# A hybrid encoder layer: pacing the merges' loads, pausing the convolutions, and masking on GpSimd

## The chip, the cores and the metric

The kernel runs on one core of one Trainium2 chip. The metric is the device time in microseconds of one execution. Engines are called PE (TensorE, with its weight loads shown apart as PEld), DVE (VectorE), ACT (ScalarE), POOL (GpSimd) and SP (SyncE, which issues nearly all DMAs here).

## The reference: one encoder layer over two sequences

A prompt of 1024 tokens and a sample of 2048 tokens, each with 16 learned meta tokens in front, go through one layer with a model width of 1024:

```
xn   = rmsnorm(h, g_pre)
proj = xn @ w_in + b_in            # 6672 columns: q, k, v, z of the attention; q/k, v, z, o, gates of the mLSTM; merge gates
ya   = (neighbourhood_attention(na_q, na_k, na_v, na_rpb) * silu(na_z)) @ w_a
yb   = (mlstm(silu(conv3(ml_qk)), ml_v, ml_g, ml_o) * silu(ml_z)) @ w_b
y    = (sigmoid(mg_a) * ya + sigmoid(mg_b) * yb) @ w_out
out  = h + rmsnorm(y, g_post)
```

The attention looks at a window of 8 rows by 16 columns on a grid 64 columns wide, and at the meta tokens. The mLSTM is a gated recurrence, run forwards and backwards, computed here in chunks of 128 tokens with a triangular mask inside a chunk: for the forward direction a key position s counts for a query position t where s <= t, for the backward direction where s >= t. A depthwise convolution of three taps precedes its q and k. All is float32.

## The kernel before: a dense stream and a sparse stream, interleaved by hand

**Products.** Float32 accuracy comes from splitting each operand into a high part (float32r) and the rest; a product is three matmuls, high x high, high x low, low x high (`mm3`, L178 to L182). So nearly every operand goes once through ACT (the high part, a copy) and once through DVE (the rest, a subtraction): weights L283 and L284, activations L526 and L527, branch outputs L1980 and L1964.

**Order.** The order of PE's instructions is the order in which the Python program issues them. Two generators make it: `dense` walks through `PLAN` (input projections, then six finals), and `sparse` through `STEPS` (mLSTM of the prompt, attention of the prompt, mLSTM of the sample, attention of the sample). `run` advances them in turn by estimated costs. The order of the other engines' instructions, and of SyncE's DMA issues, is found by the framework's scheduler from simulated times; an instruction may float forward when its inputs are ready early. `behind` pins an instruction behind everything issued before it on the same engine. On the chip each queue is worked off in order.

**The seven-product stage.** The prompt's remaining columns are computed by a seven-product scheme in place of eight block products (`sstream`; the first operands are loaded in `sbegin` while the last ordinary projection job runs, in `group`). Its products are numbered 1 to 7 and come in the order 1, 6, 5, 2, 7, ... Between the products `beside` is called once per turn: it advances the convolutions of the mLSTM's q and k (`pstep` advances one of two active `cprep` generators: a load L1579, an ACT pass L1584, DVE passes L1587, a tanh L1589, a DVE pass L1591, a store L1597), background work, and stores of split activations. The prompt's 32 convolution pieces are queued at the third job of the first projection group.

**The mLSTM.** Per head, states are computed over all blocks of 256 tokens, then outputs (`ml_outputs`). For each block a tile `um` is loaded two blocks ahead (L1758, broadcast from DRAM), `mask` adds the triangular mask of 0 and -1e30 to it on DVE (L1780, 128 x 512 elements, both directions), and `decay` takes its exponential on ACT (L1786). The prompt has 4 blocks a head, the sample 8, with 4 heads each.

**The finals.** Each of the six finals takes 512 tokens: two of the prompt, four of the sample. A final has a merge (eight output tiles, each with a product for either branch, L180 to L182 with `yh` and `yl`, then the gates: L2033 to L2037) and an output projection (`prods`, L2066 to L2068: 4 column groups x 2 halves x 4 token tiles, 32 steps). The branch outputs are eight tiles of 256 KB: `yload` loads them (L1960), and splits one at a time, seven of its own turns after the load at the earliest. It is started in the output projection of the final before, after the sixth step, and advanced once a step. In its first turn it issues every load whose data exist. The gate tiles `tg` (256 KB, L2005) are loaded for three output tiles when a merge begins, and from then on three tiles ahead; they have four buffers for each branch. Neither kind of load is pinned. Beside the finals runs the sample's attention, whose `na_prep` loads queries, keys (`kr`, L1343 and L1344), values (`vr`, L1348 and L1349) and biases for each head on the same queue, with one buffer for `kr` and one for `vr`.

## Time and profile before

| | us |
|---|---|
| median of 3 runs | 2712.46 |
| lowest and highest run | 2709.28, 2717.65 |
| the profiled execution | 2722.07 |
| its span, first to last instruction | 2720.3 |
| PE busy | 2674.3 |
| DVE busy | 1791.8 |
| ACT busy | 1547.3 |
| POOL busy | 125.3 |
| seven-product stage begins | 202 |
| sample's mLSTM | 1424 to 1973 |
| finals | 1999 to 2712 |
| sample's attention | 2021 to 2629 |

The profile is one execution. A busy time is the union of an engine's instructions; matmuls are pipelined, so a busy PE may still run below its best. The chain of waits follows the work that ended last backwards, at each step to what released it; a row has its start, its duration and what it was. In rows of windows the figures behind the span's length are the busy times of PE, PEld, DVE, ACT and POOL with their counts of instructions, then the granted TensorE clock, the mean busy share of the core's 16 DMA engines, and what they moved in GB/s. A row of waits has the total, the number of times and the longest. A row of one tile's instructions has the shortest, median and longest duration in ns, and the first and last start in us.

### The profile page before, as it was taken

What the parts mean: (1) busy time and instruction counts of PE and PEld (TensorE: products, weight loads), DVE (VectorE), ACT (ScalarE), POOL (GpSimd) and SP (SyncE); (2) the same over time, 40 slices, a digit from 0 to 9 for tenths busy, and PEclk for the clock granted to TensorE, in tenths of its full rate; (3) what the DMA queues carried; (4) which work ended last, traced back from release to release, by engine and by line L of the source; (5) the groups of instructions that cost most, each with busy time, mean ns of one, the idle gap of its engine ahead of it and who ended that gap; (6) DMA issues with size and microseconds to landing.
All of it is one profiled execution on the core that took longest, in us unless ns stands there. A gap on an engine that the chain in (4) does not pass through costs nothing.

```text
span 2720.3 us, 47309 instructions
## 1 busy us (share of the span) xinstructions
PE 2674.3 (98%) x16504; PEld 2380.2 (87%) x16504; DVE 1791.8 (66%) x4424; ACT 1547.3 (57%) x3471; POOL 125.3 (5%) x294
## 2 busy tenths in 40 slices
PE   9999999999999999999999999999999999999998
PEld 7999988879998789998878888888889898889888
DVE  5547765535777747775424858575768868687764
ACT  5233354435566656666534857575758677677641
POOL 0005000005000014000000000000000000000000
PEclk9999999999999999999999999999999999999999
DMA  9884454369765797756486656785599989798955
GB/s 371 336 283 141 139 188 157 102 238 342 268 228 184 241 320 222 230 183 226 155 287 192 224 201 214 266 284 188 175 335 335 310 270 291 237 328 245 306 202 220
DMA packets 351219, 657.26 MB, mean 242 GB/s; under 512 B 53412, under 2 KB 158580, under 8 KB 350980
## 3 DMA queue, kind: packets, MB, share of 16 engines
q1 hardware_dynamic: 343716, 645.19, 71.3%
q0 software_dynamic: 7264, 9.04, 1.2%
q8 instruction: 130, 2.13, 0.3%
q14 instruction: 109, 0.89, 0.1%
HBM read 438.38 MB, written 215.66 MB: 240 GB/s over the span
## 4 chain that ended last, share of the span: by engine, by line
PE 84%; DMA 9%; DVE 4%; ACT 2%; issue 1%; SPq 0%; POOL 0%; DVEq 0%; ACTq 0%; POOLq 0%
PE pj L180 14%; PE pj L181 13%; PE pj L182 13%; PE pj L658 5%; PE pj L659 5%; PE pj L660 5%; PE sm L1424 2%; PE pj L2066 2%; PE pj L2068 2%; PE pj L2067 2%; PE tr L1410 2%; DMA wraw<-wu 1%; DMA tg<-gt 1%; DMA vr<-nv 1%; PE pa L1852 1%
## 5 line engine op out<-in xcount | busy, mean ns | idle before, releaser
L180 PE MATMUL pj<-xh,whi 128*128 128x512 f32 (+1 forms) x1480 | 580.8, 392 | 5.2 <-ACT st L581 3.9
L181 PE MATMUL pj<-xl,whi 128*128 128x512 f32 (+1 forms) x1480 | 566.2, 383 | 0.4 <-DVE xl L357 0.4
L182 PE MATMUL pj<-xh,wlo 128*128 128x512 f32 (+1 forms) x1480 | 565.3, 382 | 0.2 <-DVE wlo L284 0.2
L658 PE MATMUL pj<-whi,xh 128*128 128x256 f32 (+1 forms) x1152 | 330.8, 287 | 0.0
L182 PEld LDWEIGHTS pj<-xh,wlo 128*128 128x128 f32 x1480 | 278.5, 188 | 58.1 <-DVE wlo L284 0.4
L180 PEld LDWEIGHTS pj<-xh,whi 128*128 128x128 f32 x1480 | 278.5, 188 | 55.0 <-ACT st L581 4.7
L659 PE MATMUL pj<-wlo,xh 128*128 128x256 f32 (+1 forms) x1152 | 324.9, 282 | 0.0
L660 PE MATMUL pj<-whi,xl 128*128 128x256 f32 (+1 forms) x1152 | 324.8, 282 | 0.0
L181 PEld LDWEIGHTS pj<-xl,whi 128*128 128x128 f32 x1480 | 279.0, 189 | 46.4 <-issue 0.7
L2066 PE MATMUL pj<-whi,mh 128*128 128x256 f32 x768 | 221.9, 289 | 0.0
L2067 PE MATMUL pj<-wlo,mh 128*128 128x256 f32 x768 | 218.4, 284 | 0.0
L2068 PE MATMUL pj<-whi,mlo 128*128 128x256 f32 x768 | 218.4, 284 | 0.0
L658 PEld LDWEIGHTS pj<-whi,xh 128*128 128x128 f32 x1152 | 217.2, 189 | 0.4
L659 PEld LDWEIGHTS pj<-wlo,xh 128*128 128x128 f32 x1152 | 217.1, 188 | 0.2
L660 PEld LDWEIGHTS pj<-whi,xl 128*128 128x128 f32 x1152 | 217.1, 188 | 0.0
L1413 DVE TENSOR_TENSOR pts<-tr,pts 96x384 fp32r<-96x384 f32 (+2 forms) x192 | 118.6, 618 | 65.4 <-ACT pts L1412 64.6
L180 PE MATMUL pj<-yh,whi 128*128 128x512 f32 x384 | 154.1, 401 | 0.7 <-ACT yh L1436 0.7
L181 PE MATMUL pj<-yl,whi 128*128 128x512 f32 x384 | 151.0, 393 | 0.2 <-DVE yl L1437 0.2
L182 PE MATMUL pj<-yh,wlo 128*128 128x512 f32 x384 | 151.0, 393 | 0.0
L2067 PEld LDWEIGHTS pj<-wlo,mh 128*128 128x128 f32 x768 | 147.6, 192 | 1.0
L2066 PEld LDWEIGHTS pj<-whi,mh 128*128 128x128 f32 x768 | 147.6, 192 | 1.0
L2068 PEld LDWEIGHTS pj<-whi,mlo 128*128 128x128 f32 x768 | 147.4, 192 | 0.0
(460 smaller groups left out, 6150.8 us busy)
## 6 DMA issues: line engine op xcount, KB each, us to landing
whi<-wh SPq DMA_DIRECT2D x140, 512.0 KB
wlo<-wl SPq DMA_DIRECT2D x140, 512.0 KB
wraw<-wu SPq DMA_DIRECT2D x64, 512.0 KB
wh<-whi SPq DMA_DIRECT2D x64, 512.0 KB
wl<-wlo SPq DMA_DIRECT2D x64, 512.0 KB
gt<-st SPq DMA_DIRECT2D x96, 256.0 KB
tg<-gt SPq DMA_DIRECT2D x96, 256.0 KB
xt<-xt SPq DMA_DIRECT2D x32, 512.0 KB
```

The source lines that it names most:

```text
L180: mm(out, ah, bh, start=start, stop=False, **more)
L181: mm(out, ah, bl, start=False, stop=False, **more)
L182: mm(out, al, bh, start=False, stop=stop, **more)
L658: nc.tensor.matmul(o, xh, wh, start=k == 0 and not (pair and a), stop=False, skip_group_check=True)
L659: nc.tensor.matmul(o, xh, wl, start=False, stop=False, skip_group_check=True)
L660: nc.tensor.matmul(o, xl, wh, start=False, stop=k == KT - 1, skip_group_check=True)
L1410: nc.tensor.transpose(pt[:ks, ch, :], pr_[:, ch * ks:(ch + 1) * ks], self.ident)
L1413: nc.vector.tensor_tensor(pts[:ks, :nb, 1, :], pt[:ks, :nb], pts[:ks, :nb, 0, :].bitcast(F32), op=ALU.subtract)
L1424: nc.tensor.matmul(av[:, cb % 2], vt[:ks, kc // 8 + ch].rearrange("p a b -> p (a b)"), pts[:ks, ch].rearrange("p a b -> p (a b)"), start=c ...
L2066: nc.tensor.matmul(o, mh[:, f, xs], q, start=fresh and f == 0, stop=False, skip_group_check=True)
L2067: nc.tensor.matmul(o, mh[:, f, xs], w[1][:, k, :], start=False, stop=False, skip_group_check=True)
L2068: nc.tensor.matmul(o, ml[:, f, xs], q, start=False, stop=f == KT - 1, skip_group_check=True)
```

## The change

Three edits:

- The convolutions pause: `quiet` is set when the last projection job before the seven-product stage begins, and cleared at the first product 7; while it is set, `beside` advances no convolution.
- The mask of the sample's mLSTM (`s` is 1) is made by two selections on POOL, one for either direction, 2 x 128 elements per partition each, which write -1e30 where the position lies outside the triangle. The prompt's mask stays an addition on DVE.
- `yload` pins its loads and issues at most one per turn, at every second turn, unless the merge already needs it (`need`). Gate tiles are pinned as well; the first three output tiles' six gate tiles of a following final are asked for in the second half of the output projection before it, one at every second step. The first final has none asked for ahead and loads them when its merge begins, as before.

```diff
     def beside(self):
 
         self.turn += 1
-        self.pstep()
-        if (1, 0) in self.have:
+        for _ in range(0 if self.quiet else 1 + ((1, 0) in self.have)):
             self.pstep()
...
             if u == 7 and not n:
+                self.quiet = False
                 self.sbload(1)
...
                 elif last and nxt and nxt[0] == "S":
                     if hf == 0:
+                        self.quiet = True
                         while self.bg:
...
         def mask(b):
             if b < NB:
-                self.behind(nc.vector.tensor_tensor(ums[b], ums[b], self.trim, op=ALU.add))
+                if not s:
+                    self.behind(nc.vector.tensor_tensor(ums[b], ums[b], self.trim, op=ALU.add))
+                    return
+                for d in range(2):
+                    u = ums[b][:, :, d]
+                    nc.gpsimd.affine_select(u, u, [[0, CB], [1 - 2 * d, P]], ALU.is_ge, -BIG, base=0, channel_multiplier=2 * d - 1)
...
         def load(k):
-            nc.sync.dma_start(yl[:, k].bitcast(F32), self.YA[s][b][k][:, :] if k < 4 else self.YB[s][k - 4][:, b * n:(b + 1) * n])
+            self.behind(nc.sync.dma_start(yl[:, k].bitcast(F32), self.YA[s][b][k][:, :] if k < 4 else self.YB[s][k - 4][:, b * n:(b + 1) * n]))
             todo.append((k, step + 7))
...
         while todo or late or half is not None:
+            idle = True
             for k in tuple(late):
                 if (("ml", s) if k > 3 else ("na", s, b, k)) in self.done:
-                    late.remove(k)
-                    load(k)
+                    idle = False
+                    if step % 2 == 0 or self.need:
+                        late.remove(k)
+                        load(k)
+                    if not self.need:
+                        break
             if half is not None:
                 low(half)
                 half = None
-            idle = True
...
-        tgs = {}
+        tgs, self.tgs = self.tgs, {}
+
+        def gate(tgs, ft, br, s, t0):
+            tg = fp.tile([P, n], F32, name="tg", tag=("st", "stT")[br], bufs=4)
+            self.behind(nc.sync.dma_start(tg, self.GT[s][8 * br + ft][:, t0:t0 + n]))
+            tgs.setdefault(ft, []).insert(0, tg)
 
         def gates(ft):
-            if ft < KT:
-                tgs[ft] = []
+            if ft < KT and ft not in tgs:
                 for br in (1, 0):
-                    tg = fp.tile([P, n], F32, name="tg", tag=("st", "stT")[br], bufs=4)
-                    nc.sync.dma_start(tg, self.GT[s][8 * br + ft][:, t0:t0 + n])
-                    tgs[ft].insert(0, tg)
+                    gate(tgs, ft, br, s, t0)
...
+        ahead = deque((ft, br) for ft in range(3) for br in (1, 0)) if nxt and nxt[0] == "f" else ()
         for cq in range(4 if nxt else 2):
...
                     if hook:
                         next(hook, None)
+                    if ahead and cq > 1 and tt % 2:
+                        gate(self.tgs, *ahead.popleft(), nxt[1], n * nxt[2])
                     yield 12 * C256
```

More of the change, by code (lines that the diff above doesn't have):

```diff
@@ L144, in __init__ @@
         self.hold, self.early = deque(), True
-        self.rpre, self.xhold = {}, True
+        self.rpre, self.xhold, self.quiet, self.tgs = {}, True, False, {}
     def rsqrt8(self, pool, v, shape):
```

## The prediction, on record before the result

> **What bounds the kernel now.** I read the page first, then the waits of PE, the chain of waits, the windows, and the rows of the tiles that the change touches. The page says that TensorE is the bound:
>
> ```profile
> span 2720.3 us, 47309 instructions
> ...
> PE 2674.3 (98%) x16504; PEld 2380.2 (87%) x16504; DVE 1791.8 (66%) x4424; ACT 1547.3 (57%) x3471; POOL 125.3 (5%) x294
> ```
>
> The matmuls are the same before and after, in the same order, so an edit can only shorten what PE loses: its idle time, 2720.3 - 2674.3 = 46.0 us, and time at a reduced clock. Part of that is the opening and the end, which no edit touches. The largest idle times are in the last third, where the six merges and output projections run beside the second neighbourhood attention. Waits of PE between 2180 and 2600 us (total, times, longest):
>
> ```profile
> PE sm L1424 <- ACT prb L1393: 7.0, 2, 5.7
> PE sm L1424 <- DVE pts L1413: 3.5, 1, 3.5
> PE sm L1424 <- DVE yg L1431: 2.2, 2, 2.0
> ```
>
> All three stand before the attention's last product. ACT and DVE are only the last links; the chain of waits shows what held them (start, duration, what):
>
> ```profile
> 2177.90 8.15 DMA yl<-yb
> 2186.11 7.41 DMA kr<-nk
> 2193.54 8.33 DMA vr<-nv
> ...
> 2209.74 1.13 PE sm L1424 x4
> ...
> 2322.12 8.37 DMA kr<-nkm
> ...
> 2337.39 1.01 PE sm L1424 x3
> ...
> 2566.05 5.39 DMA tg<-gt
> 2571.46 10.47 DMA vr<-nv
> ...
> 2584.02 0.74 PE sm L1424 x4
> ```
>
> Each time the attention's next keys or values (kr, vr) land late, behind loads for the next merge (yl, its branch outputs; tg, its gates). The queue at the first of the three, as SyncE issued it, and the load on the DMA engines early and late in that projection (the last two figures are DMA share and GB/s):
>
> ```profile
> 2174.72 3.49 SPq L1960 DMA_DIRECT2D yl<-yb  x4
> 2179.19 2.52 SPq L1960 DMA_DIRECT2D yl<-ya  x3
> 2182.76 0.45 SPq L1342 DMA_DIRECT2D qr<-nq  x1
> 2183.39 2.14 SPq L2005 DMA_DIRECT2D tg<-gt  x3
> ```
>
> ```profile
> 2170.00:2191.00 21.00, 21.00 (x172) 20.66 (x171) 15.76 (x37) 16.97 (x38) 0.00 (x0) 1.00 1.03 362
> 2191.00:2213.00 22.00, 20.00 (x151) 19.60 (x150) 13.78 (x32) 15.94 (x37) 0.00 (x0) 0.93 1.00 291
> 2213.00:2236.00 23.00, 23.00 (x188) 22.71 (x187) 16.03 (x37) 19.04 (x43) 0.00 (x0) 1.00 0.79 234
> ```
>
> Seven yl loads and three tg loads leave within 11 us, right when the projection starts, and its first two thirds run with the DMA engines full; the last third has a fifth to spare. After each stall the clock is lowered (the figure before the DMA share):
>
> ```profile
> 2209.80:2213.20 3.40, 3.40 (x16) 3.40 (x17) 1.65 (x4) 2.22 (x7) 0.00 (x0) 0.50 0.77 302
> 2336.10:2342.90 6.80, 5.51 (x25) 5.51 (x26) 5.10 (x13) 6.16 (x18) 0.00 (x0) 0.50 0.90 264
> 2585.30:2588.70 3.40, 3.40 (x17) 3.37 (x16) 2.83 (x6) 2.95 (x9) 0.00 (x0) 0.50 1.01 323
> ```
>
> At half clock half of the stretch is lost: (3.4 + 6.8 + 3.4) / 2 = 6.8 us. The three stalls cost 5.7 + 3.5 + 2.0 = 11.2 us, so together 18.0 us are at stake here.
>
> **Part 1, the merges' loads.** The bytes stay. Each yl load is now pinned behind what was traced on SyncE before it, and one goes at every second turn of the loader's generator instead of all at once. That generator is advanced once in each of an output projection's 32 steps from the sixth on. By the windows above a projection takes about 66 us, so a step is 2.06 us and the eight loads leave over 15 steps, some 31 us, instead of at once. Six gate tiles go, pinned too, in the projection's second half, at every second step. So kr and vr of the attention share the engines with one 256 KB load per 4 us and no longer queue behind ten. What is late next: the last yl load leaves at turn 14, its split is due at turn 21 and ends at 22, of 27 (0 to 26); four steps, 8 us, are left, and the loads quoted land in 5 to 11 us, well inside the 7 turns (14 us) allowed. The gates needed first were asked for 30 us ahead. The cost of the moved loads is hidden by the spare fifth of the last third. Pinning puts nothing new in front of the weights, but a gate tile later in the merge can no longer slip ahead of an attention load that waits for its buffer; it is asked for three tiles ahead. Bounds: 0, if the attention's loads stay late by themselves, to -18.0 us. I take two thirds, **-12.0 us**, because the three chains pass through yl or tg, but the engines stay nearly full and a smaller wait may remain in each.
>
> **Part 2, the pause.** In the stretch where the seven-product stage starts (202 us), PE waits for a weight split that DVE does between convolution passes:
>
> ```profile
> PE pj L1097 <- DVE wlo L273: 1.8, 2, 1.1
> ```
>
> ```profile
> 202.00:225.00 23.00, 21.21 (x173) 20.22 (x172) 20.81 (x26) 12.39 (x18) 0.00 (x0) 1.00 0.47 147
> 225.00:432.00 207.00, 207.00 (x1338) 187.41 (x1337) 146.89 (x236) 89.91 (x144) 36.47 (x72) 1.00 0.53 167
> ```
>
> DVE is 90% busy there (20.81 of 23.00). The pause lasts from the last projection job to the stage's fifth product, 32 + 16 turns, and takes away the convolutions' ACT and DVE passes and their loads and stores on SyncE. They come back later, beside the 207 us in which PE never waits and DVE is 71% busy: the same passes at the same pace, ending some 70 us later, my estimate from the stretch that they skip. Nobody reads them before the stage ends. Bounds 0 to -1.8 us; I take **-1.8 us**.
>
> **Part 3, the masks.** 32 of the 48 additions L1780 leave DVE (4 heads of 8 blocks), and 64 selections of 256 elements per partition come to POOL:
>
> ```profile
> L1780 DVE TENSOR_TENSOR um<-um,trim x48: 668/685/693, 648.6 to 1945.9; 128x512 f32<-128x512 f32 x48
> ```
>
> ```profile
> 1508.00:1605.00 97.00, 94.93 (x492) 79.31 (x492) 71.06 (x241) 69.85 (x183) 0.00 (x0) 1.00 0.63 209
> ```
>
> DVE is relieved of 32 x 0.685 = 21.9 us. The second row is one head's eight output blocks: PE idles 2.07 us with DVE 73% busy, so at most about 2 us a head can come of it. No selection stands in the trace; the nearest rows are POOL's copies:
>
> ```profile
> L1195 POOL CAST xmm<-xl x1: 288/288/288, 5.0 to 5.0; 128x128 fp32r<-128x128 f32 x1
> ```
>
> ```profile
> L599 POOL COPY km<-st x4: 190/194/1197, 161.7 to 181.8; 128x16 f32<-128x16 f32 x4
> ```
>
> From 16 elements (190 ns) to 128 (288 ns) is 0.875 ns an element, so 256 take some 0.40 us, my estimate; the upper end is the longest copy, 1.20 us. Two selections are then 0.8 to 2.4 us a block on an engine with nothing else to do there. The tile is loaded two blocks ahead, so ACT's exponentials need not wait. But the longest copy tells more:
>
> ```profile
> 180.56 2.35 DVE L789 TENSOR_TENSOR r1l<-xt,r1h 128x1024 fp32r<-128x1024 f32 x2
> ```
>
> ```profile
> 181.77 1.20 POOL L599 COPY km<-st 128x16 f32<-128x16 f32 x1
> ```
>
> It ends at 182.97, 0.06 us after DVE's subtraction of two SBUF tiles (182.91): POOL was held for as long as DVE ran. The Trainium skill, "SBUF — State Buffer", section "SBUF: two separate sides", has the rule: a GpSimd instruction that reads SBUF and a VectorE instruction with two SBUF inputs exclude each other for a whole instruction, whichever starts first. By that rule DVE would wait up to 64 x 0.40 = 26 us for 21.9 us saved, and the masks' gain would be nothing; the trace agrees as far as POOL waiting goes, and no run here shows DVE waiting. The gain is bounded by the idle time, 4 x 2.07 = 8 us; the loss by the slower rival on POOL below. I take **-1.0 us**: a copy that was held for a whole subtraction makes it likely that much of the time saved comes back as waiting on one side or the other.
>
> **Sum.** -12.0 - 1.8 - 1.0 = -14.8 us for the profiled execution, 2722.07 us, which becomes 2707.3. That execution is 9.6 us above the runs' median (2712.46). If all of this excess sits in the three stalls, the runs hold only 18.0 - 9.6 = 8.4 us of them; if none, 18.0. I take the middle, 13.2, and two thirds of it, 8.8 us: 2712.46 - 8.8 - 2.8 = **2701 us**.
>
> **Rivals.** *Nothing to speak of.* The bursts were not the cause: kr and vr keep landing late because weights, outputs and residuals alone fill the engines (share 1.00 where only three of ten burst loads were still being issued). Then a quarter of 13.2 us goes, 2712.5 - 3.3 - 2.8 = 2706 us. For it speaks the full DMA share; against it, that the last third of the projection, without yl and tg, shows 0.79 and no stall. Chance 0.28.
>
> *All of it.* The runs hold all 18.0 us and lose them: 2712.5 - 18.0 - 2.8 = 2692 us. Chance 0.16.
>
> *Slower: POOL holds VectorE up in the long mLSTM.* By the row above DVE has (97 - 71.06) / 8 = 3.2 us to spare a block. If each selection takes S and DVE waits it out, DVE loses 2S - 0.685 a block; this decides from S = 1.95 us. At 2.40 us, twice the longest copy, 0.9 us a block are left over, x 32 = 29 us, on 2702 without the masks' gain: 2731 us. For it speaks the copy that took six times its 0.19 us; against it the 0.40 us estimate. Chance 0.09.
>
> *Slower: the paced loads come too late.* If a yl load lands more than the 14 + 8 us after its turn, the merge waits. One stall as large as the worst row (5.7 + 3.4 us) in each of five merges is 45 us, less the gain: 2746 us. It needs landings twice the longest quoted. Chance 0.05.
>
> **How the numbers follow.** The forecast itself (2695 to 2704) has the remaining 0.42. About 0.3%, 8 us, is what a measurement of this kernel can tell from no change. Faster by more: 0.42 + 0.16 = 0.58; the same: 0.28; slower: 0.09 + 0.05 = 0.14. The range goes from below "all of it", 2689, with another 3 us of the masks' bound, to 2715, past "nothing to speak of" by one row's noise (the three runs span 8.4 us); the slower cases are left out.
>
> **What would show it.** Right: the three waits at L1424 under 1 us each, the granted clock 1.00 through the projections; yl issues some 4 us apart and tg issues in a projection's second half; the row of L1097 gone and the last convolution pass near 500 us; 16 additions L1780 and 64 selections of about 0.4 us. Wrong: kr or vr still on the chain before a stall of over 2 us in a projection; PE waiting for a merge's gates or split outputs at its start; selections over 1.9 us, with DVE's two-input passes longer or idle behind them.

## The result: slower by 0.4%, and the profile after

| | before | after |
|---|---|---|
| median, us (10 runs of each, side by side) | 2716.98 | 2727.53 |
| lowest and highest, us | 2709.28, 2720.06 | 2721.63, 2732.95 |
| ratio to before, with its 95% interval | | 1.0041 [1.0031, 1.0052] |
| the profiled execution, us | 2722.07 | 2725.81 |

The ten runs of before here were taken beside those of after; ratios below are to such runs, not to the three of the table of before. The ratios leave out a few disturbed executions, longer by more than 150 us; a median given in us may include one.

The page of after: the matmuls are as many as before and stand in the same order. DVE has 32 instructions fewer and POOL 64 more. POOL is busy for 28 us more. DVE's passes add up to 21.7 us less, but since successive passes overlap in the records, its busy time falls by 10 us only:

```profile
span 2724.0 us, 47409 instructions
...
PE 2677.2 (98%) x16504; PEld 2380.5 (87%) x16504; DVE 1781.7 (65%) x4392; ACT 1546.2 (57%) x3471; POOL 153.3 (6%) x358
```

Between 2180 and 2640 us the waits of PE in after are small (total, times, longest); the three of 5.7, 3.5 and 2.0 us at the attention's last product are gone:

```profile
PE sm L1425 <- ACT prb L1394: 1.2, 1, 1.2
PE pj L180 <- ACT yh L1437: 0.7, 1, 0.7
```

But over the whole span two waits head the list that did not exist before, both for branch outputs:

```profile
PE pj L180 <- ACT yh L1990: 7.1, 1, 7.1
PE pj L181 <- DVE yl L1970: 5.6, 1, 5.6
```

They stand at the start of the first merge, at 2012 to 2026 us. SyncE's queue there in after shows why: the first final's last `yl` load was asked for in its turn, but goes out only behind the attention's loads (L1343 to L1352), because it is pinned there (first_unpinned below tests this); the gate tiles follow 4 us later.

```profile
1997.56 1.08 SPq L1966 DMA_DIRECT2D yl<-ya  x1
...
1999.21 0.48 SPq L1966 DMA_DIRECT2D yl<-ya  x1
...
2007.30 0.47 SPq L1344 DMA_DIRECT2D kr<-nk  x1
...
2013.40 0.34 SPq L1966 DMA_DIRECT2D yl<-ya  x1
...
2017.82 2.75 SPq L2012 DMA_DIRECT2D tg<-gt  x5
```

In before all eight loads were out by 1980.5 and the first gate tiles left at 2006.56. PE in after is 5.7 us behind before at this point (the first three columns of the table below), so against the matmuls the last load is some 27 us later:

```profile
1975.91 2.13 SPq L1960 DMA_DIRECT2D yl<-yb  x4
1978.56 1.96 SPq L1960 DMA_DIRECT2D yl<-ya  x4
...
2006.56 1.90 SPq L2005 DMA_DIRECT2D tg<-gt  x3
```

What the engines do with them in after (start, duration, what, and in brackets the idle time before it and its cause):

```profile
2018.98 0.63 ACT L1990 ACTIVATE yh<-yl 128x512 fp32r<-128x512 f32 x1 [10.43 <-DMA yl<-ya]
...
2024.72 0.69 DVE L2045 SCALAR_TENSOR_TENSOR tg<-tg,pj 128x512 f32<-128x512 f32 x1 [14.86 <-DMA tg<-gt]
2025.33 0.68 DVE L1970 TENSOR_TENSOR yl<-yl,yh 128x512 fp32r<-128x512 f32 x1
```

ACT makes the high part as soon as the load lands, which ends PE's first wait. The low part, a subtraction on DVE, stands in DVE's queue behind the first gate pass, and that waits for a gate tile until 2024.72. So one late load costs 7.1 us and the late gates another 5.6. The clock was at half for 17 us around these waits; the first figure behind the length is PE's busy time:

```profile
2015.20:2032.20 17.00, 6.93 (x15) 5.09 (x16) 5.15 (x7) 4.01 (x6) 0.00 (x0) 0.50 0.89 308
2170.00:2260.00 90.00, 90.00 (x654) 84.97 (x653) 71.39 (x171) 70.18 (x161) 0.51 (x1) 1.00 1.00 300
```

The second row is the stretch of the projection that had the first stall: PE never waits and the clock is full.

In the sample's mLSTM the mask's rows are as announced (shortest, median, longest in ns), 64 selections and 16 additions:

```profile
L1786 POOL TENSOR_SCALAR_AFFINE_SELECT um<-um x64: 401/407/858, 1454.2 to 1946.2; 128x256 f32<-128x256 f32 x64
...
L1782 DVE TENSOR_TENSOR um<-um,trim x16: 670/683/692, 645.2 to 909.6; 128x512 f32<-128x512 f32 x16
```

But ACT, which takes the exponential of the mask, now stands waiting. In after, 1424 to 1985 us:

```profile
ACT um L1792 <- POOL um L1786: 45.2, 28, 4.4
```

and in before, in the same stretch:

```profile
ACT um L1786 <- DVE um L1780: 3.1, 8, 0.9
```

**Where the time went.** Since PE's order is the same in every kernel of this study, the start of one and the same matmul can be compared between two traces. The table gives, for stretches bounded by five such matmuls (those that start at 225, 1424, 1985, 2050 and 2690 us in before), how much longer (+) a stretch took than in before's profiled execution. Each row is one execution, so differences of one or two us in a cell are noise; in the last column it is several us, as the rows with the old loads show. The kernels below the first two rows are those of the experiments.

| kernel | to 225 | to 1424 | to 1985, the sample's mLSTM | to 2050, first merge | to 2690, other finals |
|---|---|---|---|---|---|
| before | 0 | 0 | 0 | 0 | 0 |
| after | -3.6 | +1.1 | +8.2 | +15.0 | -17.4 |
| quiet_only | -3.9 | -1.1 | +0.1 | -0.6 | -7.7 |
| masks_only | +4.6 | +1.0 | +7.2 | -0.5 | -10.1 |
| loads_only | -2.1 | -1.3 | +0.6 | +15.4 | -14.9 |
| loads_rest | -0.1 | +4.1 | 0.0 | 0.0 | -11.3 |
| quiet_loads_rest | -3.9 | -1.9 | 0.0 | +0.1 | -13.9 |
| first_free | -3.0 | -0.4 | +8.2 | +6.4 | -17.8 |
| first_unpinned | -0.9 | +1.5 | -0.2 | -0.6 | -16.9 |
| gates_ahead | +2.2 | +4.2 | -0.2 | -0.7 | -14.4 |
| masks_pin | +1.3 | +2.2 | +8.2 | -0.2 | -5.3 |
| mask_none | +2.3 | +4.1 | +11.0 | -0.1 | -7.0 |
| mask_dve_free | +0.8 | +6.2 | +14.6 | -0.4 | -7.5 |
| mask_both | +1.2 | +2.7 | +10.5 | -0.3 | -11.5 |
| masks_split | -1.1 | +1.3 | +3.1 | -0.6 | -3.4 |
| none_split | -2.1 | -0.2 | +4.1 | +0.6 | -12.5 |
| best | -3.6 | -0.5 | -0.3 | -0.7 | -16.1 |
| best_masks | -4.3 | -1.2 | +4.5 | -0.4 | -8.8 |

For after: a gain at the seven-product stage, a loss of 8 in the sample's mLSTM, a loss of 15 at the first merge, and the finals' gain. The last column also says that before's profiled execution was a bad one for the finals: the eight other kernels that load there as before stand at -3.4 to -12.5.

### The profile page after: what moved, and what is told of

Same layout as the page of the kernel before. It is cut to its first block, busy times and chain, and to the rows that moved or that the text cites. A ratio compares the mean times of both kernels' runs of the same rounds, so it can differ in the third digit from the quotient of the medians.

```text
span 2724.0 us, 47409 instructions
## 1 busy us (share of the span) xinstructions
PE 2677.2 (98%) x16504; PEld 2380.5 (87%) x16504; DVE 1781.7 (65%) x4392; ACT 1546.2 (57%) x3471; POOL 153.3 (6%) x358
## 4 chain that ended last, share of the span: by engine, by line
PE 86%; DMA 7%; DVE 3%; ACT 2%; issue 1%; SPq 1%; POOL 0%; DVEq 0%; POOLq 0%; ACTq 0%
PE pj L180 13%; PE pj L181 13%; PE pj L182 13%; PE pj L657 5%; PE pj L658 5%; PE pj L659 5%; PE pj L2079 3%; PE pj L2078 3%; PE pj L2080 3%; PE sm L1425 3%; PE tr L1411 3%; DMA um<-ud 2%; PE pa L1858 1%; PE sm L182 1%; PE sm L180 1%
```

## Experiments

### One part at a time: masks_only, loads_only, quiet_only, and first_free

**masks_only**, before with the masks alone:

```diff
         def mask(b):
             if b < NB:
-                self.behind(nc.vector.tensor_tensor(ums[b], ums[b], self.trim, op=ALU.add))
+                if not s:
+                    self.behind(nc.vector.tensor_tensor(ums[b], ums[b], self.trim, op=ALU.add))
+                    return
+                for d in range(2):
+                    u = ums[b][:, :, d]
+                    nc.gpsimd.affine_select(u, u, [[0, CB], [1 - 2 * d, P]], ALU.is_ge, -BIG, base=0, channel_multiplier=2 * d - 1)
```

> The kernel before with only the masks of the long mLSTM on POOL. Theory A: POOL is idle and the masks are off the path, so 0 +- 3 us on about 2717. Theory B: ACT's exponentials, no longer held back by a pinned DVE addition, stand early in ACT's queue and wait there for the tile's load (38.4 us of ACT waiting in the changed kernel's mLSTM), PE loses some 7 us in that stretch: 2722 to 2727 us.

Measured: 2726.82 us, ratio 1.0032 [1.0019, 1.0045]. The masks lose 9 us by themselves, and the table puts 7.2 of it in the sample's mLSTM.

**loads_only**, before with the loads' part (both `yload` and the gates, of all six finals):

```diff
-            nc.sync.dma_start(yl[:, k].bitcast(F32), ...
+            self.behind(nc.sync.dma_start(yl[:, k].bitcast(F32), ...
...
-                    late.remove(k)
-                    load(k)
+                    idle = False
+                    if step % 2 == 0 or self.need:
+                        late.remove(k)
+                        load(k)
+                    if not self.need:
+                        break
...
+            self.behind(nc.sync.dma_start(tg, self.GT[s][8 * br + ft][:, t0:t0 + n]))
...
+                    if ahead and cq > 1 and tt % 2:
+                        gate(self.tgs, *ahead.popleft(), nxt[1], n * nxt[2])
```

> The kernel before with only the paced and pinned branch loads and the gates asked for ahead (no pause, masks on DVE). Theory A: the first merge's stall of 21 us less what the five other output projections gain, 8 to 18 us: 2720 to 2730 us. Theory B: no loss here, 2700 to 2712 us.

Measured: 2725.51 us, ratio 1.0034 [1.0020, 1.0048]. The waits of PE from 1990 us on repeat those of after:

```profile
PE pj L180 <- ACT yh L1984: 7.6, 1, 7.6
PE pj L181 <- DVE yl L1964: 5.8, 1, 5.8
```

**quiet_only**, before with the pause alone:

```diff
-        self.pstep()
-        if (1, 0) in self.have:
+        for _ in range(0 if self.quiet else 1 + ((1, 0) in self.have)):
             self.pstep()
...
             if u == 7 and not n:
+                self.quiet = False
...
                     if hf == 0:
+                        self.quiet = True
```

> The kernel before with only the pause of the convolutions. Both theories: the two waits at the start of the seven-product stage go, 1.8 to 3 us, about 2714 us; a gain of nothing would mean that they are made up for later, a loss that the convolutions' later end is on the path.

Measured: 2709.78 us, ratio 0.9970 [0.9957, 0.9984]: 8 us, where 1.8 to 3 were expected. The sum of the three parts, -0.30 + 0.32 + 0.34 = +0.36%, is near after's +0.41%: the parts do not need each other for the loss.

**first_free**, after with the first final's eight branch loads all at once and unpinned, its gates still pinned:

```diff
         def load(k):
-            self.behind(nc.sync.dma_start(yl[:, k].bitcast(F32), ...
+            x = nc.sync.dma_start(yl[:, k].bitcast(F32), ...
+            if paced:
+                self.behind(x)
...
-                    if step % 2 == 0 or self.need:
+                    if step % 2 == 0 or self.need or not paced:
...
-        self.ygen = self.yload(s, b)
+        self.ygen = self.yload(s, b, (s, b) != (0, 0))
```

> The changed kernel, but the first final's eight branch loads go all at once and unpinned, as before; the other five finals keep the paced loads. Theory A (the first merge is starved: PE waits 7.1 and 5.6 us for its split outputs there, and 17 us run at half clock, some 21 us in all): 2727 - 21 = about 2706 us, 0.3 to 0.5% under the kernel before, both waits gone. Theory B (the masks on POOL are the loss, through ACT waiting for them): the first merge's stall is mostly given back later, since the finals are short of DMA and not of time, and the time stays within 5 us of 2727.

Measured: 2716.26 us, ratio 1.0000 [0.9986, 1.0013]: some 11 us better than after, with the branch loads early. That lies between the two theories: the first asked for both waits to go. What is left at the first merge is the gates' half, a wait that ends with DVE's work on `tg`:

```profile
PE pj L180 <- DVE tg L2047: 4.6, 1, 4.6
```

### The loads: which final, and is it the spacing or the pin?

**loads_rest**, loads_only with the first final as in before:

```diff
-            self.behind(nc.sync.dma_start(yl[:, k].bitcast(F32), ...
+            x = nc.sync.dma_start(yl[:, k].bitcast(F32), ...
+            if paced:
+                self.behind(x)
...
-            self.behind(nc.sync.dma_start(tg, self.GT[s][8 * br + ft][:, t0:t0 + n]))
+            x = nc.sync.dma_start(tg, self.GT[s][8 * br + ft][:, t0:t0 + n])
+            if s or t0:
+                self.behind(x)
...
-        self.ygen = self.yload(s, b)
+        self.ygen = self.yload(s, b, (s, b) != (0, 0))
```

> The kernel before with the paced and pinned loads and the gates ahead in the five later finals only; the first final loads as before, unpinned (no pause, masks on DVE). Theory C (the pacing removes stalls that really stand in the runs, and the first merge's stall alone hid it): 2717 - 8 to - 18, 2699 to 2709 us. Theory D (the three stalls are large only in that one profiled execution, or new small waits take their place): within 4 us of 2717.

Measured: 2708.73 us, ratio 0.9969 [0.9956, 0.9982]. So the five later finals gain 8.4 us, and the first one, 0.34 + 0.31 = 0.65%, costs 18 us by the runs, with an uncertainty of some 5.

**quiet_loads_rest**, the same with the pause:

```diff
                     if hf == 0:
+                        self.quiet = True
```

> The same with the pause of the convolutions as well; masks on DVE. The pause gave 0.997. Theory C: 2690 to 2702 us; theory D: as with the pause alone, 2706 to 2712 us.

Measured: 2702.27 us, ratio 0.9943 [0.9929, 0.9957]. The two gains add up.

**first_unpinned**, loads_only with the first final's loads and gates still asked for one by one, at every second turn, but not pinned:

```diff
-            self.behind(nc.sync.dma_start(yl[:, k].bitcast(F32), ...
+            x = nc.sync.dma_start(yl[:, k].bitcast(F32), ...
+            if (s, b) != (0, 0):
+                self.behind(x)
...
+            if s or t0:
+                self.behind(x)
```

> The kernel before with the changed loads in all finals (no pause, masks on DVE), but the first final's branch loads and gates are not pinned; they are still spaced, one at every second turn. Theory G (the spacing is what makes them late: the eighth load leaves only at turn 14 of 16 to 19): the wait for split outputs in the first merge stays above 3 us, 2718 to 2726 us. Theory H (the pinning is, since they stand behind attention and weight loads, and the gates hold DVE): it goes, and the time is that of the kernel with the first final as before.

Measured: 2705.85 us, ratio 0.9958 [0.9945, 0.9971]. The largest wait of PE from 1990 us on is this one, and it is not at the first merge:

```profile
PE sm L1424 <- ACT prb L1393: 1.3, 1, 1.3
```

The loads are still asked for one by one, but without the pin the scheduler moves their issues forward. They leave as in before, four and four:

```profile
1976.32 2.32 SPq L1960 DMA_DIRECT2D yl<-yb  x4
1979.16 2.04 SPq L1960 DMA_DIRECT2D yl<-ya  x4
```

So the pin is what holds the first final's loads back, and without it they are not paced either.

**gates_ahead**, before with the gates' part alone (asked for ahead, and pinned but for the first final); the branch loads go in a burst as before:

```diff
+            x = nc.sync.dma_start(tg, self.GT[s][8 * br + ft][:, t0:t0 + n])
+            if s or t0:
+                self.behind(x)
...
+                    if ahead and cq > 1 and tt % 2:
+                        gate(self.tgs, *ahead.popleft(), nxt[1], n * nxt[2])
```

> The kernel before with only the gate tiles asked for ahead and pinned (the first final's not pinned); the branch loads all at once and unpinned, as before. If the burst of eight branch loads is what holds the attention's loads up: within 4 us of 2717. If the gates in the burst are half of it: 2708 to 2713 us. With both changed it was 0.9958.

Measured: 2710.12 us, ratio 0.9974 [0.9964, 0.9984]. The gates alone bring 0.26% of first_unpinned's 0.42%. The difference, 0.16%, is about as large as the two intervals together leave uncertain, so it is not shown that the branch loads' pacing adds anything.

The traces point the same way. At the matmuls of the prediction's three waits the nine kernels with the old loads wait 1.6 to 2.1 us (first), 1.6 to 5.7 us (second), and, in three of the nine, 1.6 to 3.5 us (third). In gates_ahead none of the three is there. Its list from 1990 us on is headed by two other waits, at matmuls that stand at 2172 and 2295 us in before:

```profile
PE sm L1424 <- ACT prb L1393: 3.4, 2, 2.0
```

And yet a burst of branch loads still leaves just in front of the attention's keys in the projection of the second wait:

```profile
2306.04 3.82 SPq L1960 DMA_DIRECT2D yl<-yb  x4
2311.92 2.75 SPq L1960 DMA_DIRECT2D yl<-ya  x3
...
2317.73 0.45 SPq L1343 DMA_DIRECT2D kr<-nk  x1
```

In before three gate loads left among them; they are gone from there.

### The masks: POOL's price, DVE's, or the order on ACT?

After masks_only two theories stood: the selections hold DVE or come late themselves, or ACT's exponentials have moved. For each of the 32 blocks of the sample the traces give the time from the issue of the mask's load to the exponential. Its median is 13.3 us in before and 5.0 us in after and masks_only. In before the pinned addition starts 12.3 us after the load's issue; a selection starts at 4.5 us, most often as soon as the load has landed. So the exponential's place in ACT's queue has moved forward, to just behind the load. PE's waits that grow with it in masks_only, between 1424 and 1985 us, are those for ACT's `kt` and for `vh`, 0.5 and 0.3 us in before:

```profile
PE pa L180 <- ACT kt L1710: 2.4, 3, 1.4
PE pa L1857 <- DVE vh L1799: 2.3, 2, 1.3
```

With the 3.4 us of half clock that follow one of them, worth 1.7 us, they are 5.6 of the table's 7.2 us.

**mask_none** leaves the sample's mask out, which takes POOL's part to nothing:

```diff
                 if not s:
                     self.behind(nc.vector.tensor_tensor(ums[b], ums[b], self.trim, op=ALU.add))
-                    return
-                for d in range(2):
-                    u = ums[b][:, :, d]
-                    nc.gpsimd.affine_select(u, u, [[0, CB], [1 - 2 * d, P]], ALU.is_ge, -BIG, base=0, channel_multiplier=2 * d - 1)
```

> The kernel before with the mask of the long mLSTM left out altogether: neither DVE nor POOL makes it, so the sample's mLSTM is computed without its triangle. Theory P (POOL's selections cost the 9 us, by their latency or by the port): without them and with DVE relieved of 21.9 us, 2710 to 2717 us. Theory S (the selections cost nothing; the pinned DVE addition is missing, and the scheduler's other order of DVE and ACT costs the 9 us): the loss stays although nothing has taken its place, 2722 to 2728 us.

Measured: 2726.44 us, ratio 1.0034 [1.0022, 1.0046]. With no mask to make, the loss is all there, and ACT now waits for the load itself:

```profile
ACT um L1787 <- DMA um<-ud: 44.4, 19, 6.4
```

**mask_dve_free** keeps the sample's mask on DVE as in before and only takes its pin away:

```diff
-                self.behind(nc.vector.tensor_tensor(ums[b], ums[b], self.trim, op=ALU.add))
+                x = nc.vector.tensor_tensor(ums[b], ums[b], self.trim, op=ALU.add)
+                if not s:
+                    self.behind(x)
```

> The kernel before with the long mLSTM's masks on DVE as they were, but not pinned. Theory S in the form that the pin is what holds things in place: the additions float forward to the tile's simulated landing and DVE waits there, 2720 to 2728 us. Theory P: no change, within 4 us of 2717.

Measured: 2737.91 us, ratio 1.0068 [1.0055, 1.0081]: the worst of all, with no POOL in it. The exponentials come 5.2 us after the load, as in after: it was the pin on the addition that had kept them back. But the additions have floated forward as well, and DVE now waits for the loads too:

```profile
DVE um L1780 <- DMA um<-ud: 59.0, 26, 5.0
```

So this run has two queues waiting and does not tell ACT's part from DVE's; mask_none, in which ACT alone waits, does.

**masks_pin** pins the exponentials where the program issues them:

```diff
-                        nc.scalar.activation(ums[b][:, j, d], ums[b][:, j, d], AF.Exp, bias=g[d]["a"][:, 1 + b * CB + j, h:h + 1])
+                        x = nc.scalar.activation(ums[b][:, j, d], ums[b][:, j, d], AF.Exp, bias=g[d]["a"][:, 1 + b * CB + j, h:h + 1])
+                        if s:
+                            self.behind(x)
```

> The kernel before with the masks of the long mLSTM on POOL, and the exponentials behind them on ACT pinned to their place in the program. Theory E (the loss of the masks comes from the exponentials, which float forward in ACT's queue and stand there waiting for the tile's load, some 38 us in the changed kernel): the ACT waits on POOL fall under 10 us and the loss of 0.32% goes, 2714 to 2720 us. Theory F (POOL itself costs it, by the port that it shares with DVE): the loss stays, 2723 to 2728 us, and DVE passes with two SBUF inputs are longer than in the kernel before.

Measured: 2728.01 us, ratio 1.0035 [1.0022, 1.0049]. No gain: ACT no longer waits for POOL, but the exponential now comes 21.8 us after the load and 2.9 us (median) before its use, and PE waits for the product behind it:

```profile
PE pa L1859 <- ACT sh L1841: 4.7, 2, 3.4
```

**mask_both** keeps the pinned addition and adds the selections, which then change nothing:

```diff
                 self.behind(nc.vector.tensor_tensor(ums[b], ums[b], self.trim, op=ALU.add))
+                for d in range(2 * s):
+                    u = ums[b][:, :, d]
+                    nc.gpsimd.affine_select(u, u, [[0, CB], [1 - 2 * d, P]], ALU.is_ge, -BIG, base=0, channel_multiplier=2 * d - 1)
```

> The kernel before, masks pinned on DVE, and both selections on POOL behind them on the same tile (their result is the same, so they are work for nothing on the path from the addition to the exponentials). Theory P: as with the masks on POOL or worse, 2725 to 2735 us. Theory S: the order of DVE is as before, so within 4 us of 2717.

Measured: 2724.19 us, ratio 1.0026 [1.0016, 1.0035], between the two theories. The exponentials keep their place (13.9 us after the load), and ACT waits 8.4 us in all for POOL behind DVE. What reaches PE is chiefly a wait for `hl`, 1.6 us in before:

```profile
PE pa L1855 <- DVE hl L1860: 5.6, 2, 3.2
```

So the distance to the load is not all. Whether POOL's work has a price here this run does not say; the same wait appears below with no mask at all.

**masks_split** has the selections, and holds the exponentials on ACT behind the copy of the same block's q and k, the work that they followed in before:

```diff
-                nc.scalar.activation(z[:, :, :, 0], raw, AF.Copy)
+                copies[b] = nc.scalar.activation(z[:, :, :, 0], raw, AF.Copy)
...
-                for d in range(2):
-                    for j in range(CB):
-                        nc.scalar.activation(ums[b][:, j, d], ...
+                with self.tc.issue_after(copies[b].ins) if s else ExitStack():
+                    for d in range(2):
+                        for j in range(CB):
+                            nc.scalar.activation(ums[b][:, j, d], ...
```

> The kernel before with the long mLSTM's masks on POOL and the exponentials held behind the same block's copy of q and k on ACT (median before: 2.7 us behind it; with the masks on POOL alone 6.1 us ahead of it, pinned in the earlier run 10.5 us behind it). Theory S (the loss is the exponentials' place in ACT's queue): ACT's waits for the masks fall under 10 us and the loss goes, 2710 to 2719 us. Theory P (POOL's own work costs it): 2722 to 2728 us whatever the place.

Measured: 2718.99 us, ratio 1.0007 [0.9996, 1.0018]. ACT's wait is gone, and most of the 0.32% with it:

```profile
ACT um L1792 <- POOL um L1785: 0.5, 1, 0.5
```

**none_split** is masks_split without any mask for the sample:

```diff
-                for d in range(2):
-                    u = ums[b][:, :, d]
-                    nc.gpsimd.affine_select(u, u, [[0, CB], [1 - 2 * d, P]], ALU.is_ge, -BIG, base=0, channel_multiplier=2 * d - 1)
```

> The same place of the exponentials, but the long mLSTM's mask left out altogether, on either engine. Theory S: 2708 to 2717 us; the distance to the run with POOL's masks is POOL's own price. Theory P: at least 6 us under the run with POOL's masks.

Measured: 2719.73 us, ratio 1.0005 [0.9994, 1.0016]. The same as with the selections, though 3 us more than the theory of the order had asked for: POOL's work costs nothing here that the runs can tell, and DVE's 21.9 us saved bring nothing. Both kernels still show 3 to 4 us in the mLSTM's column of the table. It is chiefly one wait, in masks_split:

```profile
PE pa L1858 <- DVE hl L1863: 4.1, 2, 3.6
```

In none_split it is 4.0 us, in before 1.6. It comes without the mask too, so it belongs to the order that results, not to POOL.

The traces show which order. The long wait stands before the same matmul in masks_split, none_split, best_masks and mask_both; in before that matmul starts at 1662 us. PE waits for DVE's addition `hl`, and that for ACT's copy `hl`. In before ACT makes the copies `ss` and `hl` first and then `hb`, four passes of the output's normalisation:

```profile
1660.66 0.36 ACT L1823 ACTIVATE ss<-sc 128x256 f32<-128x256 f32 x1
1660.93 0.37 ACT L1856 ACTIVATE hl<-pa 128x260 f32<-128x260 f32 x1
1661.19 1.64 ACT L1938 ACTIVATE hb<-hb,nb,nwy 128x128 f32<-128x128 f32 x4
```

In masks_split `hb` has slipped in front of them:

```profile
1661.34 1.65 ACT L1944 ACTIVATE hb<-hb,nb,nwy 128x128 f32<-128x128 f32 x4
1662.88 0.38 ACT L1829 ACTIVATE ss<-sc 128x256 f32<-128x256 f32 x1
1663.14 0.39 ACT L1862 ACTIVATE hl<-pa 128x260 f32<-128x260 f32 x1
```

none_split and best_masks have masks_split's order, and in mask_both the copy `hl` stands behind `hb` too. The wait is 2 us longer than in before, and 3.4 to 6.8 us of half clock follow it, so it is about what the table's column shows for masks_split, none_split and best_masks. This is read from the traces; no run held `hb` back to test it.

### The versions that the experiments point to

**best**: first_unpinned with the pause; the masks are as in before.

```diff
                     if hf == 0:
+                        self.quiet = True
```

> The pause and the changed loads, with the first final's loads and gates spaced but not pinned, masks on DVE. If the pause (0.997) and the loads (0.9958) add up: 0.9928, about 2697 us; if they remove the same time, as the one of them does when the finals' waits move by chance: 2702 to 2706 us.

Measured: 2702.12 us, ratio 0.9939 [0.9927, 0.9951], against 0.9928 by adding up, which the interval just includes.

**best_masks**: best with masks_split's masks.

```diff
-                self.behind(nc.vector.tensor_tensor(ums[b], ums[b], self.trim, op=ALU.add))
+                if not s:
+                    self.behind(nc.vector.tensor_tensor(ums[b], ums[b], self.trim, op=ALU.add))
+                    return
+                for d in range(2):
+                    u = ums[b][:, :, d]
+                    nc.gpsimd.affine_select(u, u, [[0, CB], [1 - 2 * d, P]], ALU.is_ge, -BIG, base=0, channel_multiplier=2 * d - 1)
...
+                with self.tc.issue_after(copies[b].ins) if s else ExitStack():
```

> The fastest version so far (pause, changed loads, the first final's not pinned; 0.9939) with the masks on POOL and the exponentials behind the copy of q and k. Theory S: the masks cost nothing any more and give back a little of DVE's 21.9 us, 2696 to 2703 us. Theory P: 2707 to 2713 us.

Measured: 2707.92 us, ratio 0.9965 [0.9952, 0.9977], 5.8 us behind best and inside the range of the theory that POOL costs the time. But the table puts 4.8 of that in the mLSTM, where the `hl` wait stands (3.7 us, with 6.8 us of half clock behind it), and none_split has it without POOL. The selections gain nothing in either place.

## Why the prediction was wrong, point by point

**Part 1, the stalls at stake: the place and the size right, the cause half right.** In after the three waits are gone, the clock is full through the projections, `yl` issues are 4.5 us apart on average in the first projection (2199.95 to 2231.19 for eight), and the five later finals give 8.4 us [4.9, 11.9] in the runs of loads_rest where 8.8 was forecast (first_unpinned, which treats these five alike, gives 11.4, so that the two lie so near is partly luck). But the prediction held the burst of ten loads to be the cause, seven of them branch loads. gates_ahead keeps the branch loads' burst and has none of the three waits: moving the gates is enough, and a gain from pacing the branch loads is not shown. One reading for the rival "nothing to speak of" was wrong too: in the row with a DMA share of 1.00 none of the ten burst loads was still being issued, the last of them left by 2185.53. The guess that before's profiled execution had an excess in these stalls holds too: the medians of the table's last column are -7.5 for the old loads and -15.5 for the new (without gates_ahead), 8 apart, while the profile of before alone would have given 15.5.

**Part 1, "what is late next": the step that failed.** The working counted turns of an output projection (27, with 8 us to spare) and said that the gates needed first were asked for 30 us ahead. Both hold for five merges of six. The first final has no output projection before it. Its loader is advanced in the last projection job alone, by 16 to 19 turns, of which eight loads at every second turn take 15; and it has no gates asked for ahead, as the description of the change itself says. "Pinning puts nothing new in front of the weights" looked at what the pin puts in front of others, not at what it puts in front of the pinned load: the attention's loads of its first head. The last load left some 27 us later than in before, PE waited 7.1 + 5.6 us, and the stretch took 15 us longer. The rival "the paced loads come too late" had this mechanism, at 0.05, and looked for it in the five merges where it did not happen.

**Part 2: the right place, and under-sized.** The stage's waits are gone in all six kernels with the pause. The term of 1.8 us was one execution's idle time of PE, and this stall differs between executions: in the twelve without the pause PE waits 1.1 to 4.1 us between 195 and 230 us, with a median of 2.2, and in four of them the clock falls behind it. gates_ahead, which is the same kernel up to there, has one of the largest:

```profile
PE pj L1096 <- DVE sn L975: 2.1, 1, 2.1
PE pj L1097 <- DVE wlo L273: 2.0, 2, 1.1
```

```profile
204.00:212.00 8.00, 4.82 (x39) 4.28 (x38) 4.68 (x8) 4.29 (x7) 0.00 (x0) 1.00 0.62 202
212.10:215.50 3.40, 3.40 (x16) 3.40 (x17) 3.40 (x5) 3.40 (x5) 0.00 (x0) 0.50 0.39 118
```

Even before's own stretch from 202 to 225 us is 2.5 us shorter with the pause, not 1.8. Over the twelve executions without the pause the table's first column has a median of 0.4 us, over the six with it -3.8: 4.1 us, of which the matmuls between 202 and 225 us make 2.8. In the second column the medians are +1.9 and -0.8, another 2.7 us, for which the prediction had no term; there one wait, at the transposition of the prompt's last heads near 960 us, is 1.1 to 2.5 us in all twelve traces without the pause and absent in all six with it. In before ACT stood there behind a convolution of the sample whose load was late. That adds up to 6.8 us, inside the runs' 0.30% [0.16, 0.43], 8 us. Why the pause moves that convolution's load was not tried. The convolution passes of the prompt came back beside hidden work as forecast, the last of them at 497 us.

**Part 3: the selection's price right, the conclusion wrong.** The estimate of 0.40 us a selection measured 0.407. The step that failed is "ACT's exponentials need not wait". It asked when the data are there, not where the instruction stands. The scheduler lets an instruction float forward to where its simulated inputs are ready, and what stands behind it in the queue then waits with it; the addition on DVE, which was pinned, had been holding the exponential back by some 8 us. With the pin gone ACT waited 45 us in all for masks whose loads had not landed, and that reached PE chiefly as the waits for `kt` and `vh`. masks_split and masks_only tell this apart from all that POOL does: with the same selections, 1.0007 against 1.0032; and so do none_split and mask_none without any, 1.0005 against 1.0034. No rival of the prediction said it.

**The lock between POOL and DVE: there, and small.** In masks_only some selections take twice their 0.407 us, and some of DVE's subtractions of two SBUF tiles half as long again:

```profile
L1799 DVE TENSOR_TENSOR vh<-va,vh x31: 397/422/650, 1496.9 to 1978.5; 128x260 fp32r<-128x260 f32 x31
```

```profile
L1785 POOL TENSOR_SCALAR_AFFINE_SELECT um<-um x64: 401/407/866, 1462.9 to 1953.3; 128x256 f32<-128x256 f32 x64
```

The longest of these subtractions in before is 430 ns. The Trainium skill, "SBUF — State Buffer", section "SBUF: two separate sides", says that either may hold the other for a whole instruction; here the trace agrees in kind, on both sides. By that rule DVE could have lost 26 us; its two-input passes together grew by about 3 us over the mLSTM (by 0.2 us in none_split, which has no selections), and none_split against masks_split shows no price that the runs can tell. The prediction cut the masks' gain from 8 us at most to 1.0 for this lock. No gain came, but the lock is not shown to have taken it: in none_split, without selections, there is none either.

**The sum.** Parts by the runs: pause -8.2 us, masks +8.7, loads +9.2 (the later finals -8.4, the first +18); together +10, measured +11 [8, 14].

**What stays open.** Whether holding `hb` behind the copies `ss` and `hl` would bring masks_split and best_masks level with the kernels that keep the pinned addition, and what part of mask_both's 0.26% is POOL's. What the pacing of the branch loads is worth by itself is open too.

## What to carry to other kernels

A pin on an in-order queue works in both directions: before pinning a load, write down what stands in front of it at each place where the code runs, and check the first and the last iteration on their own, since "one load every second turn" needs turns that only the middle ones have. Before moving an operation off an engine, ask what its place in the order was holding: if a consumer was kept back by it, give the consumer an anchor of its own in the same edit (here: behind the copy that it followed), and measure with the operation left out altogether to see whether its work or its place was what counted. Take a part of a change away by itself before naming it as the cause: the gates did what had been put down to the branch loads. And read a stall's size from several executions: one stall was 1.1 to 4.1 us in twelve of them, and the profile of before showed twice of another.

## What the runs showed of the hardware

**A stall of half a clock window costs twice, and whether it does is a matter of phase.** The starts of the half-clock stretches in one trace differ by whole multiples of 3.413 us: in gates_ahead 212.1, 877.7 and 928.9 us are 195 and 15 windows apart. Laying that grid over all 18 traces: of the windows at full clock between 150 and 2690 us, all 53 with more than 1.90 us of idle PE were followed by half clock, none with less than 1.41 us was, and between these both occur. Two stalls of 1.24 and 0.91 us, 0.47 us apart, at the same matmuls near 872 us in every kernel, were followed by half clock in 9 of 18 traces: in those in which both fell into one window, or nearly so. gates_ahead has them in one window (PE busy for 1.26 of 3.41 us), and the next runs at half:

```profile
874.30:877.70 3.40, 1.26 (x6) 0.64 (x5) 3.16 (x5) 3.10 (x6) 0.00 (x0) 1.00 0.91 290
877.70:881.10 3.40, 3.40 (x12) 2.92 (x13) 2.45 (x6) 1.28 (x5) 0.00 (x0) 0.50 0.98 336
```

quiet_only has the same two stalls on either side of a window's border, and keeps its clock:

```profile
867.09:870.50 3.41, 2.10 (x10) 1.27 (x8) 3.13 (x5) 3.41 (x6) 0.00 (x0) 1.00 0.89 234
870.50:873.91 3.41, 2.58 (x14) 2.27 (x15) 3.39 (x8) 1.97 (x7) 0.00 (x0) 1.00 1.00 326
```

The Trainium skill, "TensorE: Matmul & The Clock Gate", section "Part 1: The HAM clock gate (the "warmup" mystery)", describes a free-running window of 3413 ns, and the grid agrees; it lets the clock fall after a whole idle window, and here a little over half of one was enough. The grid stands anywhere against a kernel's first instruction: its first border comes 0.05 to 3.22 us behind it in the 18 traces. So the same stall costs 1.7 us more in one execution than in the next, and part of what a single profile shows of it is luck.
